# A transformer layer on one core: x times eleven weight blocks as seven products of quarters, interleaved with query/key tiles

## The chip, the cores and the metric

The kernel runs on one core of a Trainium2 chip. The metric is device time in microseconds of one execution. The engines are TensorE (PE, matmuls into PSUM), VectorE (DVE), ScalarE (ACT), GpSimd (POOL) and SyncE (SP, which here only issues transfers). Everything in and out is float32.

## The reference

One layer for 256 tokens of width 2048. `x @ w_in` gives queries, keys and values of three dilated attention groups of eight heads, the queries, keys (1024 columns each), values and output gate (2048 each) of a gated linear attention (GLA), a small decay input, and two gates m_a and m_b of 2048. Both attentions are projected, gated and summed, then follow an output product, a layer norm, a convolutional feed-forward network (FFN) of 5632, and a second layer norm:

```
parts = split(x @ w_in)
o_g, lse_g = dilated attention of group g, 8 heads            # g = 0, 1, 2
ya = (softmax over g of lse_g weighs o_g) @ w_proj_a
o  = GLA(q, k, v, decay), normalised per head
yb = (o * silu(gr)) @ w_proj_b
x1 = layernorm(ALPHA * x + (sigmoid(m_a) * ya + sigmoid(m_b) * yb) @ w_out)
h  = silu(conv3(x1 @ w_gate) + b) * (x1 @ w_up)
out = layernorm(ALPHA * x1 + h @ w_down)
```

## The kernel before

A float32 value is split into two float32r parts, `hi` (ACT copies the value into the narrower type) and `lo` (DVE subtracts `hi` from it), and a product is made of three matmuls: hi by hi, hi by lo, lo by hi. `x` lies split in on-chip memory for the whole first half. Weights come from `wp`, an array of pieces of 128 x 2048 float32 (1 MB) in the order of use. `piece()` (L135) takes the next one: SP loads it into `raw` (three buffers), and `split` (L114) makes `whi` on ACT and `wlo` on DVE (two buffers each).

Two kinds of product use the pieces. In `b16` and `b_tile` (L181 to L193) the weight piece is the stationary operand, for 128 output columns: 16 matmuls of 512 columns (`x` hi and lo side by side, L185) and 16 of 256 columns (L187); `b_sum` (L228) adds the two halves, ACT copying one and DVE adding. In `a_chunk` (L242) x is stationary and the weight moves, 512 output columns for two halves of the tokens: four pieces, 96 matmuls of 512 columns (`a_part`, L238 to L240).

The order is: values `v` of four heads for three groups by `a_chunk`, then 24 query/key tiles `qk` by `b16`, and the same again for the other four heads; 16 tiles `gqk`; `gv` and `gr` (4 chunks each) by `a_chunk`; then for each of four column blocks two `m` chunks (the gates), `yp` (projection a, 8 rows of 128) and `pb` (projection b); `wo`; the first norm; the FFN, in parts FSPLIT = (20, 20, 4) of its 44 blocks, each part's gate and up tiles followed by its share of the down product `wd`; the second norm. Values, queries, keys and results stay on chip.

Smaller work is a list of closures, `side`; `pump()` (L153) takes the next one, after each tile or piece, so that its matmuls fall between the large ones. `attend` (L317) gives a head's bias fetch, scores, softmax, transposes (`turn`) and weighted sums (`mix`), with queries, keys, values and probabilities in split form; `gla` (L473) gives `gate`, `decay`, `keys`, `att` and `outs` of a GLA head, whose last matmuls (`patt`, `pgo`) take plain float32 operands.

The framework sets each engine's order at build time from the order in which instructions are written (an earlier one has priority where both could go) and from when buffers come free, and it writes the waits. Each engine then works through its own list in that order. A tile's buffer, of a tag with a fixed count, is taken again when all that use the older tile are done. PSUM has four banks for large products (`psm`) and four for the rest (`psx`).

## Time and profile before

| | |
|---|---|
| median of 3 runs | 1894.65 us (1894.32 to 1896.28) |
| profiled execution | 1894.34 us; span of its instructions 1892.5 us |
| granted TensorE clock, mean | 0.997 |
| transfers | 359 MB, mean 190 GB/s |

In the rows of the profile, "x" gives a count of instructions and "mean ns" the time of one. Matmuls overlap one another, so that the sum of their durations is more than the time that they take together; the spacing of their starts is read from the chain or the timeline. `<-` names what ended an engine's idle time.

| stage (main product) | from, us | to, us |
|---|---|---|
| v, query/key and gqk tiles, attention | 8.8 | 533.7 |
| gv, with GLA | 533.7 | 650 |
| gr | 650 | 738.8 |
| m, yp, pb | 738.8 | 1047 |
| wo, first norm | 1047 | 1143.2 |
| FFN, last norm | 1143.2 | 1892.5 |

### The profile page before, as it was taken

What the parts mean: (1) busy time and instruction counts of PE and PEld (TensorE: products, weight loads), DVE (VectorE), ACT (ScalarE), POOL (GpSimd) and SP (SyncE); (2) the same over time, 40 slices, a digit from 0 to 9 for tenths busy, and PEclk for the clock granted to TensorE, in tenths of its full rate; (3) what the DMA queues carried; (4) which work ended last, traced back from release to release, by engine and by line L of the source; (5) the groups of instructions that cost most, each with busy time, mean ns of one, the idle gap of its engine ahead of it and who ended that gap; (6) DMA issues with size and microseconds to landing.
All of it is one profiled execution on the core that took longest, in us unless ns stands there. A gap on an engine that the chain in (4) does not pass through costs nothing.

```text
span 1892.5 us, 22845 instructions
## 1 busy us (share of the span) xinstructions
PE 1868.8 (99%) x9510; PEld 1585.6 (84%) x9510; DVE 1098.2 (58%) x1135; ACT 864.2 (46%) x936; POOL 81.0 (4%) x115
## 2 busy tenths in 40 slices
PE   8999999999999999999999999999999999999996
PEld 6888888888877788888888887888888888888885
DVE  5566475665655455445454557766644566664567
ACT  5445445454446544343434435555533455553342
POOL 0000000001000000000000003400000000000001
PEclk9999999999999999999999999999999999999998
DMA  8655545455534455555556654855555655555551
GB/s 283 237 178 180 193 167 193 172 189 181 182 137 155 150 184 181 197 193 187 198 182 219 236 195 145 242 203 190 191 180 198 245 185 194 184 194 185 215 200 67
DMA packets 57618, 359.04 MB, mean 190 GB/s; under 512 B 7089, under 2 KB 8012, under 8 KB 16940
## 3 DMA queue, kind: packets, MB, share of 16 engines
q1 hardware_dynamic: 52908, 345.10, 51.4%
q0 software_dynamic: 4464, 12.24, 2.5%
q8 instruction: 74, 1.21, 0.3%
q10 hardware_dynamic: 144, 0.26, 0.0%
q14 instruction: 28, 0.23, 0.0%
HBM read 355.41 MB, written 3.31 MB: 190 GB/s over the span
## 4 chain that ended last, share of the span: by engine, by line
PE 97%; DVE 2%; ACT 0%; issue 0%; DMA 0%; SPq 0%; ACTq 0%; DVEq 0%
PE qk L185 9%; PE fu L185 8%; PE fg L185 8%; PE qk L187 5%; PE fu L187 4%; PE fg L187 4%; PE wd_t L239 4%; PE wd_t L238 4%; PE wd_t L240 4%; PE gqk L185 3%; PE m_t L239 3%; PE m_t L240 3%; PE m_t L238 3%; PE v_t L238 2%; PE v_t L239 2%; PE v_t L240 2%
## 5 line engine op out<-in xcount | busy, mean ns | idle before, releaser
L116 DVE TENSOR_TENSOR wlo<-raw,whi 128x2048 fp32r<-128x2048 f32 (+1 forms) x336 | 738.8, 2201 | 662.3 <-ACT whi L115 645.7
L115 ACT ACTIVATE whi<-raw 128x2048 fp32r<-128x2048 f32 (+1 forms) x336 | 616.7, 1837 | 560.8 <-PE wd_t L240 107.9
L185 PE MATMUL qk<-x,whi 128*128 128x512 f32 x768 | 184.2, 392 | 0.0
L185 PEld LDWEIGHTS qk<-x,whi 128*128 128x128 f32 x768 | 140.9, 188 | 28.0
L185 PE MATMUL fu<-x,whi 128*128 128x512 f32 x688 | 164.3, 391 | 0.0
L185 PE MATMUL fg<-x,whi 128*128 128x512 f32 x672 | 160.2, 391 | 0.0
L185 PEld LDWEIGHTS fu<-x,whi 128*128 128x128 f32 x688 | 126.4, 188 | 24.5
L185 PEld LDWEIGHTS fg<-x,whi 128*128 128x128 f32 x672 | 123.6, 188 | 24.0
L238 PE MATMUL wd_t<-whi,h 128*128 128x512 f32 x344 | 133.9, 389 | 0.0
L239 PE MATMUL wd_t<-wlo,h 128*128 128x512 f32 x344 | 133.9, 389 | 0.0
L240 PE MATMUL wd_t<-whi,h 128*128 128x512 f32 x344 | 133.8, 389 | 0.0
L187 PEld LDWEIGHTS qk<-x,wlo 128*128 128x128 f32 x768 | 98.5, 191 | 3.8
L238 PE MATMUL m_t<-whi,x 128*128 128x512 f32 x256 | 99.9, 390 | 0.0
L187 PE MATMUL qk<-x,wlo 128*128 128x256 f32 x768 | 99.7, 283 | 0.0
L240 PE MATMUL m_t<-whi,x 128*128 128x512 f32 x256 | 99.6, 389 | 0.0
L239 PE MATMUL m_t<-wlo,x 128*128 128x512 f32 x256 | 99.6, 389 | 0.0
L187 PEld LDWEIGHTS fu<-x,wlo 128*128 128x128 f32 x688 | 88.2, 191 | 3.4
L187 PE MATMUL fu<-x,wlo 128*128 128x256 f32 x688 | 89.2, 283 | 0.0
L187 PEld LDWEIGHTS fg<-x,wlo 128*128 128x128 f32 x672 | 86.2, 191 | 3.3
L187 PE MATMUL fg<-x,wlo 128*128 128x256 f32 x672 | 87.2, 283 | 0.0
L238 PE MATMUL v_t<-whi,x 128*128 128x512 f32 x192 | 75.6, 396 | 1.7 <-ACT whi L115 1.7
L238 PEld LDWEIGHTS wd_t<-whi,h 128*128 128x128 f32 x344 | 64.6, 188 | 13.4
(229 smaller groups left out, 2717.7 us busy)
## 6 DMA issues: line engine op xcount, KB each, us to landing
raw<-in_wp SPq DMA_DIRECT2D x317, 1024.0 KB, 4.8
row<-in_rows POOLq DMA_DIRECT2D x24, 256.0 KB, 5.3
raw<-in_wp SPq DMA_DIRECT2D x20, 256.0 KB, 5.7
bias<-bvd POOLq DMA_DIRECT2D x32, 96.0 KB, 2.8
xraw<-in_xt SPq DMA_DIRECT2D x8, 256.0 KB, 5.7
r<-in_xk POOLq DMA_DIRECT2D x8, 256.0 KB, 5.3
braw<-in_wp SPq DMA_DIRECT2D x8, 256.0 KB, 6.0
out<-r SPq DMA_DIRECT2D x7, 256.0 KB, 2.5
```

The lines of the kernel that those rows point to most:

```text
L115: nc.scalar.activation(hi, src, AF.Copy)
L116: engine.tensor_tensor(lo, src, hi.bitcast(F32), op=ALU.subtract)
L185: nc.tensor.matmul(ps, parts(kc)[0], opnd(kc), start=(kc == 0), stop=False)
L187: nc.tensor.matmul(ps[:, S:], parts(kc)[1], opnd(kc)[:, :S], start=False, stop=(kc == nk - 1))
L238: nc.tensor.matmul(ps, xh, hi, start=first, stop=False)
L239: nc.tensor.matmul(ps, xh, lo, start=False, stop=False)
L240: nc.tensor.matmul(ps, xl, hi, start=False, stop=last)
```

## The change

1. The products of x with the value, gate, `gv` and `gr` columns, eleven blocks of 2048 x 1024 (3, 4, 2 and 2), are made by `seven`: x, tokens by rows of the weight, is cut into quarters A11, A12, A21, A22 and the block into B11, B12, B21, B22 (1024 x 512, two pieces each), and four quarters of the result come from seven products (Winograd's form) instead of eight. Four combinations of x's quarters are made once, by `combine`, on DVE, and split. Those of the weight are made in place on DVE, piece by piece, before the split. Results are combined from PSUM on DVE.
2. These steps (`p1`, `p5`, `p67` twice, `p3`, `p4`, `p2`) alternate with the 64 tiles of queries and keys, one step and one tile, with a `pump` after each, for nine blocks. The two `gr` blocks come last, without tiles; the GLA work is pumped between their steps, two closures for each. What is left of it is issued after them (`drain`).
3. Results no longer stay on chip. `spill` writes them to the chip's DRAM and `fetch` reads them back at the place of use, both through POOL's queue; 256 KB each for most. `m` and `gr` are applied after all products of x are done.
4. Query, key, value and probability are used as float32 in the attention, without a split: one matmul where there were two, and no split of `pT`, `qk` and `v`.
5. Memory: pool `early` is closed after the products of x and `late` opened in its place; x, the combinations, later operands and `h` share eight buffers `res`; `raw` has two buffers, the seven products' pieces have six of their own (`quarter`), `whi` three, `wlo` two; PSUM has two banks for tiles (`psm`), four for `a_chunk` and `seven` (`psc`), two for the rest. POOL's descriptor memory is cut to 4096 bytes a partition.
6. The FFN is cut (16, 16, 8, 4). Its three first pieces, and the last ones of the down product, are no longer prepared ahead in separate blocks.

```diff
-FSPLIT = (20, 20, 4)
+FSPLIT = (16, 16, 8, 4)
...
+    early = ExitStack()
+    now = [early.enter_context(tc.tile_pool(name="early", bufs=1)), (15, 6, 4)]
...
+    def spill(name, src):
+        n_blk[0] += 1
+        d = dpool.tile(list(src.shape), F32, name=f"{name}_{n_blk[0]}")
+        nc.gpsimd.dma_start(d, src)
+        return d
+    def fetch(name, d, make=None):
+        b = (make or blk)(name)
+        nc.gpsimd.dma_start(b, d)
+        return b
...
+    def combine(xs, raw):
+
+        out = [res(f"comb{i}") for i in range(4)]
+        for j in range(4):
+            n_blk[0] += 1
+            f = [tmp("comb").rearrange("p (k t) -> p k t", k=2) for _ in range(4)]
+            (a11, a21), (a12, a22) = ([raw[h][:, :, t * P : (t + 1) * P] for t in range(2)] for h in (j, j + 4))
+            tt = nc.vector.tensor_tensor
+            tt(f[0], a21, a22, op=ALU.subtract)
+            tt(f[1], f[0], a11, op=ALU.subtract)
+            tt(f[2], a11, a21, op=ALU.subtract)
+            tt(f[3], a12, f[1], op=ALU.add)
+            for o, x in zip(out, f):
+                v = o.rearrange("p a (b c) -> p (a b) c", c=S)[:, 2 * j : 2 * j + 2]
+                split(v[:, :, :P], v[:, :, P:], x)
+        return out
+
...
+    def seven(name, xs, comb, i, store):
+
+        st = {}
+        a11 = lambda kc: quarter(xs, kc, 0)
+        a12 = lambda kc: quarter(xs, kc + 8, 0)
+        a22 = lambda kc: quarter(xs, kc + 8, 1)
+        z, s2, s3, s4 = ((lambda kc, c=c: comb_quarter(comb[c], kc)) for c in range(4))
+
+        def part(ps, a, raw, p, first):
+
+            hi, lo = two_parts(raw)
+            for w, which in ((hi, 0), (hi, 1), (lo, 0)):
+                for k in range(4):
+                    kc = 4 * p + k
+                    nc.tensor.matmul(
+                        ps, a(kc)[which], w[:, k * 512 : (k + 1) * 512],
+                        start=(first and w is hi and which == 0 and kc == 0),
+                        stop=(w is lo and kc == 7), skip_group_check=not first,
+                    )
+
+        def product(ps, a, raws, first=True):
+            for p, raw in enumerate(raws):
+                part(ps, a, raw, p, first)
+
+        tt = nc.vector.tensor_tensor
+
+        def add(a, b):
+            tt(a, a, b, op=ALU.add)
+
+        def get(k):
+            return load(i + k, "quarter", 6)
+
+        def p1():
+            st["T"] = [get(0), get(1)]
+            st["A"] = cbank(name + "A")
+            product(st["A"], a11, st["T"])
+            st["s"] = blk("s")
+            nc.scalar.activation(st["s"], st["A"], AF.Copy)
+
+        def p5():
+            st["B12"] = [get(2), get(3)]
+            for a, b in zip(st["T"], st["B12"]):
+                add(a, b)
+            st["D"] = cbank(name + "D")
+            product(st["D"], z, st["T"])
+
+        def p67(p):
+            def f():
+                if not p:
+                    st["B22"] = []
+                    st["B"], st["E"] = cbank(name + "B"), cbank(name + "E")
+                b = get(4 + p)
+                st["B22"].append(b)
+                add(st["T"][p], b)
+                part(st["B"], s2, st["T"][p], p, True)
+                add(st["B12"][p], b)
+                part(st["E"], s3, st["B12"][p], p, True)
+                if p:
+                    add(st["s"], st["B"])
+                    st["u"], c22 = blk("u"), blk("c22")
+                    tt(st["u"], st["s"], st["E"], op=ALU.add)
+                    tt(c22, st["D"], st["u"], op=ALU.subtract)
+                    store(1, 1, c22)
+            return f
+
+        def p3():
+            product(st["D"], s4, st["B22"], first=False)
+            tt(st["s"], st["D"], st["s"], op=ALU.subtract)
+            store(0, 1, st["s"])
+
+        def p4():
+            st["B21"] = [get(6), get(7)]
+            for a, b in zip(st["T"], st["B21"]):
+                add(a, b)
+            product(st["E"], a22, st["T"])
+            add(st["u"], st["E"])
+            store(1, 0, st["u"])
+
+        def p2():
+            product(st["A"], a12, st["B21"], first=False)
+            c = blk("c11")
+            nc.scalar.activation(c, st["A"], AF.Copy)
+            store(0, 0, c)
+
+        return [p1, p5, p67(0), p67(1), p3, p4, p2]
+
...
     def scores(g):
-                q, k = (x[hp] for x in qk[g])
+                q, k = qk[g][:, :S], qk[g][:, S:]
+                ps = bank("ps")
                 for t in range(2):
                     n = (t + 1) * P
-                    ps = bank("ps")
-                    nc.tensor.matmul(ps[:, : 2 * n], q[:, t * P : (t + 1) * P], halves(k)[:, :, :n], start=True, stop=False)
-                    nc.tensor.matmul(ps[:, n : 2 * n], q[:, S + t * P : S + (t + 1) * P], k[:, :n], start=False, stop=True)
+                    pt = ps[:, t * P : t * P + n]
+                    nc.tensor.matmul(pt, q[:, t * P : (t + 1) * P], k[:, :n], start=True, stop=True)
                     s = st["s"][t][:, g * n : (g + 1) * n]
-                    for part, rest in ((ps[:, n : 2 * n], st["T"][:, g, S - n :]), (ps[:, :n], s)):
-                        nc.vector.scalar_tensor_tensor(s, part, scale, rest, op0=ALU.mult, op1=ALU.add)
+                    nc.vector.scalar_tensor_tensor(s, pt, scale, st["T"][:, g, S - n :], op0=ALU.mult, op1=ALU.add)
...
+                nc.tensor.matmul(po, v0, p[:, :S], start=(g == 0), stop=False)
+                nc.tensor.matmul(po[:, P:], v1, p[:, S:], start=False, stop=(g == 2))
...
+    def head(h):
+        qk = [None] * 3
+        bias, scores, rest = attend(h, qk)
+
+        def f(g, which):
+            def t():
+                ps = b16("qk", xop, AT["qk", h] + 2 * g + which)
+                if not which:
+                    qk[g] = blk("qk")
+                b_sum(ps, qk[g][:, which * S : (which + 1) * S])
+                if which:
+                    if not g:
+                        side.append(bias)
+                    side.append(scores[g])
+                    if g == 2:
+                        side.extend(rest)
+            return t
+        return [f(g, which) for g in range(3) for which in range(2)]
+
+    for h in range(NH):
+        tiles.extend(head(h))
+
...
+    with tc.issue_after(loaded.ins):
+        tiles.pop(0)()
+    comb = []
+    tiles.pop(0)()
+    comb.extend(combine(X, XR))
+    steps = []
+    for g in range(3):
+        steps.extend(seven("v", X, comb, AT["v", g], to_v(g)))
+    for u in range(4):
+        steps.extend(seven("m", X, comb, AT["m", u], to(M[u // 2], u % 2)))
+    for u in range(2):
+        steps.extend(seven("gv", X, comb, AT["gv", u], to(GV, u)))
+    late = []
+    for u in range(2):
+        late.extend(seven("gr", X, comb, AT["gr", u], to(GR, u)))
+    ratio = len(tiles) / len(steps)
+    done = 0
+    for n, step in enumerate(steps):
+        step()
+        pump()
+        while done < (n + 1) * ratio and tiles:
+            tiles.pop(0)()
+            done += 1
+            pump()
+
...
     for h in range(GH):
         stages, o = gla(h)
-        side.extend(stages)
-        GV.append(evacuate("gv", a_chunk("gv", xop, 16, n_pump=2)))
-        side.append(o)
+        side.extend([*stages, o])
+    for step in late:
+        step()
+        pump(2)
     drain()
+    early.close()
+    now[:] = ctx.enter_context(tc.tile_pool(name="late", bufs=1)), (17, 10, 1)
...
+    YA2 = [res("ya") for _ in range(2)]
+    for h in range(NH):
+        y = YA2[h // 4][:, h % 4]
+        split(y[:, :S], y[:, S:], fetch("yaf", YA[h], tmp))
...
+        ws = [by_cols(piece(i)) for i in idx]
...
-    nc = bacc.Bacc("TRN2", target_bir_lowering=False, num_devices=1)
+    nc = bacc.Bacc("TRN2", target_bir_lowering=False, num_devices=1, dynamic_dma_scratch_size=4096)
```

More of the change, by code (lines that the diff above doesn't have):

```diff
@@ L378, in f @@
-                nc.tensor.matmul(po[:, S + P :], v1[1], p[:, 0, S:], start=False, stop=(g == 2))
-                if g == 2:
-                    f32 = tmp("yaf")
-                    b_sum(po, f32)
-                    y = blk("ya", F32R)
-                    split(y[:, :S], y[:, S:], f32)
-                    YA[h] = y
-            return f
-        return bias, [scores(g) for g in range(3)], [soft(0), soft(1), turn(0), turn(1), mix(0), turn(2), mix(1), mix(2)]
-    def both(a, b):
-        for x, y in zip(a, b):
-            side.extend([x, y])
@@ L645, in hybrid_layer @@
     R = [[], []]
-    stats = [tpool.tile([P, 4, 6], F32, tag=f"st{t}", name=f"st{t}", bufs=1) for t in range(2)]
+    stats = [now[0].tile([P, 4, 6], F32, tag=f"st{t}", name=f"st{t}", bufs=1) for t in range(2)]
     def mean_and_scale(t):
```

444 lines of the change are left out of this document (223 added, 221 removed).

## The prediction

> **What bounds the kernel now.** I read the page's busy times first, then what TensorE (PE) waited for, then busy time by stage.
>
> ```profile
> span 1892.5 us, 22845 instructions
> PE 1868.8 (99%) x9510; PEld 1585.6 (84%) x9510; DVE 1098.2 (58%) x1135; ACT 864.2 (46%) x936; POOL 81.0 (4%) x115
> ...
> PE pbias L301 <- DMA oh<-in_onehot: 3.1, 1, 3.1
> PE v_t L238 <- ACT whi L115: 1.7, 1, 1.7
> ...
> core 0: us, PE busy (x) PEld busy (x) DVE busy (x) ACT busy (x) POOL busy (x), PEclk, DMA share, GB/s
> 8.80:533.70 524.90, 524.89 (x2888) 457.62 (x2889) 320.98 (x418) 253.88 (x303) 22.24 (x42) 1.00 0.56 196
> 533.70:650.00 116.30, 115.97 (x535) 89.68 (x534) 63.47 (x73) 66.94 (x107) 1.63 (x4) 1.00 0.41 145
> 738.80:1047.00 308.20, 308.20 (x1377) 255.56 (x1376) 149.31 (x89) 121.81 (x83) 2.19 (x4) 1.00 0.55 195
> 1876.40:1892.50 16.10, 0.03 (x1) 0.00 (x0) 10.56 (x14) 1.31 (x3) 4.20 (x3) 0.59 0.36 130
> ```
>
> From 8.8 to 1876 us PE never stops; its longest waits are 3.1 and 1.7 us, both at the start. The other engines are hidden beneath it, so time comes off only by taking PE work away, and the change can lose time only by making PE wait. VectorE (DVE), at 58%, is next in line.
>
> **What the change takes from PE.** Busy time is no price here, because matmuls overlap. The spacing is:
>
> ```profile
> 26.15:47.90 21.75, 21.75 (x97) 18.02 (x96) 1.38 (x2) 1.18 (x2) 1.00 0.72 254
> ...
> 195.02 1.92 PE qk L187 x16
> 196.94 0.11 PE ppt L360
> 197.05 0.22 PE ppt L363 x2
> 197.27 3.65 PE qk L185 x16
> ...
> L238 PE MATMUL m_t<-whi,x 128*128 128x512 f32 x256 | 99.9, 390 | 0.0
> L238 PE MATMUL v_t<-whi,x 128*128 128x512 f32 x192 | 75.6, 396 | 1.7 <-ACT whi L115 1.7
> L238 PE MATMUL gv_t<-whi,x 128*128 128x512 f32 x128 | 50.6, 395 | 0.0
> L238 PE MATMUL gr_t<-whi,x 128*128 128x512 f32 x128 | 50.1, 391 | 0.0
> ```
>
> One 512-column matmul every 21.75/96 = 0.2267 us (the first row is the v_t tile alone); one query/key tile is 3.65 + 1.92 = 5.57 us. The eleven blocks are these four tiles: (256+192+128+128) x 3 lines = 2112 matmuls, 192 a block. Seven products of quarters are 7 x 8 x 3 = 168 a block, 1848 in all. The 264 saved are 59.9 us.
>
> Float32 attention changes PE little. The float32 product that exists already is `pgo`, at two records a matmul:
>
> ```profile
> 570.33 1.72 PE pgo L558 x4
> 572.05 0.86 PE pgo L560 x2
> ...
> 114.89 0.12 PE ps L337
> 115.02 0.06 PE ps L338
> 115.08 0.29 PE ps L337
> 115.37 0.12 PE ps L338
> ```
>
> 512 columns cost 0.86 us, so 256 + 128 columns cost 0.645 us, against 0.59 in the last four rows. `mix` has the same column counts as those rows, 0.53 at the spacings above (0.2267 + 0.12 + 0.12 + 0.06). So +0.05 and +0.12, 24 times: +4 us. The profiled execution is 1894.34 us (span plus 1.8; the median of the runs shown is 1894.65), so with PE as full as now: 1894.34 - 59.9 + 4 = 1838.5 us. The rest of the sum is PE waiting.
>
> **What it puts on DVE.**
>
> ```profile
> L116 DVE TENSOR_TENSOR wlo<-raw,whi 128x2048 fp32r<-128x2048 f32 x316 | 725.6, 2296 | 656.8 <-ACT whi L115 640.3 <-ACT pa L230 9.5 <-PE ps L337 4.1
> L115 ACT ACTIVATE whi<-raw 128x2048 fp32r<-128x2048 f32 x316 | 604.6, 1913 | 553.2 <-PE wd_t L240 107.9 <-PE m_t L240 85.3 <-PE gqk L185 46.0
> L608 DVE TENSOR_TENSOR sg<-sg,gr_t 128x512 f32<-128x512 f32 x8 | 5.5, 688 | 4.7 <-ACT sg L607 4.6
> ...
> 197.05 2.29 DVE L116 TENSOR_TENSOR wlo<-raw,whi 128x2048 fp32r<-128x2048 f32 x1 [2.36 <-ACT whi L115]
> 199.26 0.42 DVE L231 TENSOR_TENSOR qkf<-qk,pa 128x256 f32<-128x256 f32 x1
> 199.60 0.55 DVE L116 TENSOR_TENSOR pT<-ppt,pT 128x384 fp32r<-128x384 f32 x1
> ...
> 75.80:533.70 457.90, 10.62 (x72) 8.43 (x72) 46.53 (x128) 13.12 (x32) 1.00 0.52 183
> 533.70:650.00 116.30, 38.02 (x18) 0.00 (x0) 1.00 0.41 145
> ...
> 639.23 0.63 PE patt L541 x4
> 648.59 0.86 PE pgo L560 x2
> ```
>
> Start to start, a 128x2048 operation is 2.21 us and a 128x256 one 0.34; a 128x512 one I take at 0.61 (0.69 less the same 0.08). The seven products turn the 8 splits of a block into 14 and add 8 sums of weight quarters of the same shape (twice two in `p67`, two each in `p5` and `p4`; in place, taken at the split's price), and 5 sums of 128x512 results: 22 x 2.21 + 5 x 0.61 = 51.7 us a block, where PE needs 38.1.
>
> Main loop (nine blocks' 63 steps in turn with the 64 tiles). DVE: 9 x 51.7 = 465; tiles 64 x 2.55 = 163; attention 29 (the tile `s` row, 46.5 us, without its 48 of 96 score additions, for seven heads); `combine` and x, 32 operations of 0.34 and 8 of 0.61, 16. That is 673 us. PE: 64 x 5.57 + 63 x 5.44 + 7 heads x 5 (0.645 x 6 + 0.33 x 3) = 734 us. DVE stands at 92%. ACT has 1.91 a split, so about 60%. Within a block DVE needs, with its tile, 7.5 us in `p1`, 12 in `p5` and in the first `p67`, 14 in the second, 8 in `p3`, 12.5 in `p4`, 7.5 in `p2`, against 11.7 on PE each time. It falls behind by about 3 us and gets it back. Two `wlo` buffers let it be one piece ahead, and a piece's low part is needed only after its high-part matmuls (1.8 us for a quarter, 3.65 for a tile), so the 3 us are covered. I put 8 us (1%) on waits that line up badly; ends 0 and 60.
>
> Late stage (the two `gr` blocks, with `gla` between the steps and no tiles). DVE: 2 x 51.7 + 25.4 for `gla` (63.47 less the splits' 38.02 in the window 533.7 to 650) + 4 for the last head = 133 us. PE: 76 for 28 quarters, 29 for `gla` and `pgl` (116.3 less 384 x 0.2267), 5 for the last head = 110. Here DVE is the bound: +23 us. The side list adds more: it gives 13 steps for each head's 12 chances, so some 16 are left for this stage; with 20 of `gla` against 28 chances, 8 remain when the last product is issued, and the last heads' chain (`keys`, `att`, `outs`) runs after it with little beside it. The last two rows show that chain for the last head now: from its first `patt` to its last `pgo` 10.2 us; with about half of a head's 6.4 us of DVE ahead of it, and the second head partly behind the first, some 16 us, of which a part fills gaps: +12 (ends 5 and 25).
>
> Then `early` closes, and all that `late` holds lies where it lay. If its first buffer waits for the last of `early`, the last `spill` must land, and `yaf` be fetched and split, before `yp` can start:
>
> ```profile
> r<-in_xk POOLq DMA_DIRECT2D x8, 256.0 KB, 5.3
> out<-r SPq DMA_DIRECT2D x7, 256.0 KB, 2.5
> raw<-in_wp SPq DMA_DIRECT2D x317, 1024.0 KB, 4.8
> POOL r L702 <- DMA row<-in_rows: 29.4, 8, 4.4
> ...
> 0.00:20.00 20.00, 15.19 (x48) 9.80 (x49) 10.18 (x17) 11.55 (x18) 2.80 (x15) 1.00 0.86 280
> ```
>
> 2.5 + 5.3 + issue and split about 2: +10 us (ends 0, if buffers are reused one by one, and 13). POOL has some 150 such transfers where it had 74, each of them ahead of its need by a step (11 us) in the main loop, and the PE steps behind it wait only if that lead is gone: I take 0, end 30. The fourth row shows such a wait, 4.4 us at the longest.
>
> Start. At 280 GB/s the first tile needs all of x and one piece, 3 MB in 11 us, then 1 MB for 5.6 us of PE, then 2 MB for p1; before, 1.5 MB fed each 5.4 us. PE has done some 5.6 us where it had done 9 by 18 us, waits 3 for the second piece, and `combine` (11 us of small operations ahead of p1's low parts) takes 1 or 2 more: +8 (ends 4 and 14). FFN's three first pieces are split after the norm, 5.7 us of ACT, where one of them was ready before it: +2 (ends 0 and 5). FSPLIT with one part more leaves the matmul count, and adds 8 accumulations of 0.69 on an idle DVE: 0. SP's weight loads keep their bytes: blocks load 8 MB as before.
>
> **Sum:** 1838.5 + 8 + 8 + (23 + 12 + 10) + 2 = 1901.5, so 1902 us, 0.4% above now. The saving on PE is real and is paid back, mostly in the two last blocks.
>
> **A rule that speaks against it.** The clock row: over the idle end (1876.4 to 1892.5) PE was granted 0.59, and 1.00 in every busy stage shown. The Trainium skill, "TensorE: Matmul & The Clock Gate", Part 1, says that the clock falls to half after an idle window of about 3.4 us and takes as long of work to come back. The trace agrees with the first half; no row shows a short stall. By that rule only the wait at the change of pools is long enough, an estimate of 2 us more, 1904.
>
> **Rivals.**
> 1. *The waits are filled: faster.* The order is set ahead of time, and an operation emitted later may fill a gap. If `late` reuses buffers one by one, `yp` (42 us of PE) covers the chain of `gla` and its spill; then the late stage costs 23 + 5, the start 4, the main loop 3, FFN 0: 1838.5 + 35 = 1874, up to 1890 with half of the rest. For it: DVE has 61 us of slack in the main loop, and before it never held PE. It decides when the losses stay under 52 us in all. 0.36.
> 2. *DVE bounds the main loop too: much slower.* It has 262 large operations in 734 us and 61 us of slack, 0.23 us each. Before, each split waited 640/316 = 2 us for its high part; that cost nothing with 42% idle. If 0.45 us of it stays for each, PE loses 262 x 0.45 - 61 = 57 us more: 1959. Against it: sums and the tile's split can be put between. 0.14.
> 3. *Spills and fetches hold PE through POOL's queue,* which is in order: 30 us more, 1932. 0.07.
> 4. *The clock goes to half in the late stage,* where PE stops often though briefly: its 110 us become 220, 87 over DVE's 133: 1989. The page's rule would need longer gaps than 1 to 2 us. 0.03.
>
> **How the numbers follow.** My own case, 1892 to 1918, has 0.40; it is the likeliest. 0.2% (3.8 us) is about what a measurement of this kernel can tell from no change, so its lowest part, 1892 to 1898.4, is "same": 0.13. Faster 0.36 is rival 1; slower the remaining 0.51. The range 1866 to 1945 leaves out the bottom of rival 1, the upper part of 2, and 4: under 0.2. The likeliest case's own range is 1892 to 1918.
>
> **What would show it.** PE's matmul count in the eleven blocks 264 lower at 0.227 us; DVE near 1430 us busy. The main loop at 92% DVE with PE full would hold the fourth term; idle PE there behind `wlo` is rival 2. In the two `gr` blocks PE waits for `wlo` with DVE full. A PE gap of over 8 us ahead of `yp`, behind `ya`'s split and a fetch, is the pool term; no gap is rival 1. I am wrong if the late stage takes under 120 us or the main loop over 780.

## The result, and the profile after

The changed kernel takes 1960.9 us (median; 1959.6 to 1962.5) where the kernel before takes 1895.1 (1894.3 to 1896.3): 1.0347 times as long, 95% interval 1.0329 to 1.0365. The forecast was 1902 with a range of 1866 to 1945. The profiled execution took 1961.5 us. Its page, with the rows that answer to those of before:

```profile
span 1959.8 us, 22945 instructions
...
PE 1859.2 (95%) x9246; PEld 1558.6 (80%) x9246; DVE 1428.3 (73%) x1225; ACT 973.5 (50%) x951; POOL 161.9 (8%) x261
...
PE   7999999999999999885799998899999999999997
...
DVE  7898988989898898994555556666545666446557
...
PEclk9999999999999999887799999899999999999998
...
L137 DVE TENSOR_TENSOR wlo<-raw,whi 128x2048 fp32r<-128x2048 f32 (+1 forms) x239 | 545.0, 2281 | 216.8 <-PE wd_t L245 53.3 <-issue 36.0 <-PE fg L214 35.4
...
L137 DVE TENSOR_TENSOR wlo<-quarter,whi 128x2048 fp32r<-128x2048 f32 x154 | 351.6, 2285 | 58.9 <-ACT whi L136 43.0 <-issue 4.2 <-PE qk L214 3.8
...
L321 DVE TENSOR_TENSOR quarter<-quarter,quarter 128x2048 f32<-128x2048 f32 x88 | 200.0, 2284 | 0.5
```

PE has exactly the 264 matmuls less that were counted (9510 to 9246), and DVE is at 1428 us, as forecast. But PE's busy time fell by 9.6 us only, where the matmuls and the attention together should have taken off 56, and its idle time grew from 24 to 101 us. Lost time thus shows in two places: as idle, and as busy time in which the same work takes longer, in part at a lower clock. The slices say where: the first, and then four from about 780 to 980 us, where PE drops to 5 and the clock to 7, and less of it at the norm and the start of the FFN (8 from 1176 to 1274 us).

The waits of PE, longest sums first (in total, times, longest), and the busy time by stage:

```profile
PE patt L689 <- DVE xk L665: 19.3, 3, 10.6
PE yp_t L244 <- ACT ya L136: 8.8, 1, 8.8
PE gqk L212 <- ACT whi L136: 5.7, 3, 3.1
PE pgo L707 <- POOL att L697: 5.7, 3, 3.5
PE vD L308 <- ACT whi L136: 4.7, 1, 4.7
PE fu L212 <- DVE yb L237: 4.6, 1, 4.6
```

```profile
core 0: us, PE busy (x) PEld busy (x) DVE busy (x) ACT busy (x) POOL busy (x), PEclk, DMA share, GB/s
0.00:100.00 100.00, 82.42 (x365) 63.81 (x366) 81.94 (x84) 52.33 (x56) 6.53 (x18) 0.95 0.66 244
100.00:765.70 665.70, 665.70 (x3425) 568.28 (x3424) 602.07 (x422) 374.99 (x302) 55.99 (x96) 1.00 0.62 223
765.70:892.00 126.30, 109.96 (x462) 83.82 (x460) 119.52 (x94) 73.31 (x78) 18.26 (x34) 0.91 0.36 129
892.00:954.50 62.50, 25.98 (x63) 14.77 (x63) 17.67 (x31) 21.45 (x52) 15.96 (x28) 0.61 0.30 108
954.50:1006.20 51.70, 50.64 (x225) 41.12 (x226) 38.36 (x47) 35.43 (x48) 18.80 (x36) 0.95 0.89 316
...
1184.30:1196.50 12.20, 7.62 (x24) 3.28 (x22) 8.02 (x16) 9.58 (x15) 0.00 (x0) 0.82 0.32 119
1196.50:1945.40 748.90, 739.20 (x3891) 636.29 (x3890) 453.54 (x455) 339.35 (x360) 37.88 (x41) 0.99 0.53 188
```

The stages are: start; main loop; the two `gr` blocks; from the last product of `gr` to the first of `yp` (I call it the gap); `yp`; the first norm; the FFN. The main loop keeps PE full with DVE at 90% (602.07 of 665.70). The gap has 62.5 us with 26 of PE, 18 of DVE and 21 of ACT: here nobody is busy. The norm took 8.3 us before and 12.2 now, the FFN 733.2 and 748.9.

What the gap waits for stands in its timeline (start, duration, engine, operation; in brackets the idle time before it and what ended it):

```profile
890.55 4.49 DVE L137 TENSOR_TENSOR wlo<-raw,whi 128x2048 fp32r<-128x2048 f32 x2
...
891.21 4.08 POOL L697 TENSOR_SCALAR_AFFINE_SELECT att<-att 128x256 f32<-128x256 f32 x1 [3.09 <-ACT att L695]
...
909.19 0.54 POOL L109 DMA_DIRECT2D sp<-c  x1 [4.33 <-ACT c L375]
910.24 1.07 POOL L114 DMA_DIRECT2D gq<-gkqs  x2 [0.51 <-issue]
...
913.31 0.69 DVE L659 SCALAR_TENSOR_TENSOR gq<-gq,ge 128x512 f32<-128x512 f32 x1 [2.14 <-DMA gq<-gkqs]
...
914.72 1.97 PE L689 MATMUL patt<-gq,xk 128*128 128x64 f32 x8 [10.55 <-DVE xk L665]
919.85 0.40 POOL L697 TENSOR_SCALAR_AFFINE_SELECT att<-att 128x256 f32<-128x256 f32 x1 [8.01 <-ACT att L695]
...
924.81 1.18 PE L630 MATMUL pz<-glp,gwp 80*128 80x256 f32 x1
...
928.16 0.55 POOL L109 DMA_DIRECT2D os<-o  x1 [2.86 <-DVE o L716]
928.70 1.07 POOL L114 DMA_DIRECT2D gq<-gkqs  x2
...
933.15 0.69 DVE L659 SCALAR_TENSOR_TENSOR gq<-gq,ge 128x512 f32<-128x512 f32 x1
...
934.55 1.97 PE L689 MATMUL patt<-gq,xk 128*128 128x64 f32 x8 [6.67 <-DVE xk L665]
...
948.06 0.55 POOL L109 DMA_DIRECT2D os<-o  x1 [2.86 <-DVE o L716]
950.92 0.17 POOL L733 MEMSET gbuf<- 128x2 f32 x3 [2.32 <-DMA os<-o]
951.43 4.25 POOL L114 DMA_DIRECT2D yaf<-yas  x8 [0.34 <-issue]
...
954.50 0.79 PE L244 MATMUL yp_t<-whi,ya 128*128 128x512 f32 x1 [8.81 <-ACT ya L136]
```

Two whole GLA heads are left after the last product, and they run one after the other, 20 us apart (`patt` at 914.7 and 934.6). A head's `gq` is issued on POOL's queue behind the writes ahead of it (`sp` in the first case, the last `os` of the head before in the second). The rows show what that costs here: DVE's operation on `gq` waits 2.14 us for the fetch in the first of the two heads, and in the second it does not wait for it, as it starts where ACT's `ge` has just ended. The rest of the 20 us is the head's own series of small operations. It begins with `pz` (924.8 in the second head, right behind the last `pgo` of the head before), takes 9.7 us to `patt`, and 11.1 more to the end of its last `pgo` at 945.7. Then comes the change of pools as the prediction had it: last write, memset at the place it frees, fetch, split, `yp`.

### The profile page after: what moved, and what is told of

Same layout as the page of the kernel before. It is cut to its first block, busy times and chain, and to the rows that moved or that the text cites. A ratio compares the mean times of both kernels' runs of the same rounds, so it can differ in the third digit from the quotient of the medians.

```text
span 1959.8 us, 22945 instructions
## 1 busy us (share of the span) xinstructions
PE 1859.2 (95%) x9246; PEld 1558.6 (80%) x9246; DVE 1428.3 (73%) x1225; ACT 973.5 (50%) x951; POOL 161.9 (8%) x261
## 4 chain that ended last, share of the span: by engine, by line
PE 47%; DVE 3%; issue 3%; DMA 2%; ACT 1%; POOL 1%; POOLq 0%; DVEq 0%; ACTq 0%; SPq 0%
PE fu L212 8%; PE fg L212 8%; PE fu L214 4%; PE fg L214 4%; PE wd_t L244 4%; PE wd_t L246 4%; PE wd_t L245 4%; DMA raw<-in_wp 2%; PE wo_t L246 1%; PE wo_t L244 1%; PE wo_t L245 1%; DVE wlo L137 1%; PE pb_t L245 1%; PE pb_t L244 1%; PE pb_t L246 1%
## 5 line engine op out<-in xcount | busy, mean ns | idle before, releaser
L137 DVE TENSOR_TENSOR wlo<-raw,whi 128x2048 fp32r<-128x2048 f32 (+1 forms) x239 | 545.0, 2281 | 216.8 <-PE wd_t L245 53.3
L136 ACT ACTIVATE whi<-raw 128x2048 fp32r<-128x2048 f32 (+1 forms) x239 | 452.7, 1894 | 485.7 <-DMA raw<-in_wp 374.8
L136 ACT ACTIVATE whi<-quarter 128x2048 fp32r<-128x2048 f32 x154 | 293.3, 1916 | 218.4 <-DVE quarter L321 120.0
L137 DVE TENSOR_TENSOR wlo<-quarter,whi 128x2048 fp32r<-128x2048 f32 x154 | 351.6, 2285 | 58.9 <-ACT whi L136 43.0
L321 DVE TENSOR_TENSOR quarter<-quarter,quarter 128x2048 f32<-128x2048 f32 x88 | 200.0, 2284 | 0.5
L212 PE MATMUL qk<-x,whi 128*128 128x512 f32 x768 | 189.1, 396 | 0.0
L244 PE MATMUL wd_t<-whi,h 128*128 128x512 f32 x352 | 137.1, 390 | 0.0
L246 PE MATMUL wd_t<-whi,h 128*128 128x512 f32 x352 | 137.0, 389 | 0.0
L244 PEld LDWEIGHTS wd_t<-whi,h 128*128 128x128 f32 x352 | 66.1, 188 | 13.9 <-ACT h L136 0.4
L246 PEld LDWEIGHTS wd_t<-whi,h 128*128 128x128 f32 x352 | 66.1, 188 | 13.8 <-DVE h L137 0.2
```

The lines of the kernel that those rows point to most:

```text
L136: nc.scalar.activation(hi, src, AF.Copy)
L137: nc.vector.tensor_tensor(lo, src, hi.bitcast(F32), op=ALU.subtract)
L212: nc.tensor.matmul(ps, parts(kc)[0], opnd(kc), start=(kc == 0), stop=False)
L244: nc.tensor.matmul(ps, xh, hi, start=first, stop=False)
L246: nc.tensor.matmul(ps, xl, hi, start=False, stop=last)
L321: tt(a, a, b, op=ALU.add)
```

## The experiments

The theory after this reading: the loss is a chain, not an engine, two GLA heads in series and then the change of pools; and smaller waits at the start, the norm and the FFN. The rival: DVE, which the sums and second splits fill, is the cause of most of it. (The letters in the quoted expectations are each run's own.)

Stage lengths, in us, from start to start of the matmuls named (gap: from the last product of `gr` to the first of `yp`; norm: last `wo` to first `fg`; FFN: first `fg` to last `wd`). Each is from one profiled execution. In the nine runs from gr_plain to start4, none of which changes the FFN's own work, the FFN lies between 743.5 and 748.9, so a few us in that column are not clear of the spread:

| kernel | median | gr | gap | norm | FFN |
|---|---|---|---|---|---|
| changed | 1960.9 | 125.8 | 63.0 | 12.4 | 748.5 |
| gr_plain | 1944.9 | 120.4 | 50.6 | 12.4 | 747.0 |
| no_sums | 1929.0 | 111.1 | 63.5 | 12.7 | 743.5 |
| ya_ahead | 1945.0 | 126.8 | covered | 12.4 | 747.4 |
| spread | 1937.4 | mixed | 18.0 | 12.3 | 746.5 |
| gp_banks | 1943.7 | 117.9 | 51.5 | 12.4 | 746.8 |
| gp_pump3 | 1925.8 | 119.7 | 34.3 | 12.4 | 748.6 |
| gp_ahead | 1924.0 | 121.0 | 34.0 | 12.4 | 745.9 |
| gp_all | 1913.2 | 125.4 | 17.2 | 12.4 | 746.2 |
| start4 | 1955.1 | 134.1 | 46.8 | 12.4 | 748.9 |
| gains_late | 1961.5 | 125.0 | 64.3 | 12.3 | 747.5 |
| best1 | 1898.2 | 129.9 | 0.2 | 12.0 | 747.4 |
| ffn_banks | 1952.9 | 125.2 | 64.4 | 12.4 | 740.2 |
| gains_dve | 1957.8 | 125.8 | 63.5 | 12.3 | 745.4 |
| norm_first | 1957.7 | 125.6 | 62.9 | 9.4 | 749.9 |
| ffn_raw | 1960.3 | 131.2 | 58.9 | 12.0 | 744.6 |
| best2 | 1889.8 | 128.3 | 0.3 | 9.4 | 741.8 |
| best3 | 1890.7 | 133.0 | 0.2 | 9.4 | 733.9 |

### Is it DVE?

**gr_plain**: the two `gr` blocks by four plain chunks, as before, with two closures to a piece.

```diff
-        late.extend(seven("gr", X, comb, AT["gr", u], to(GR, u)))
...
+    for h in range(GH):
+        pss = a_chunk("gr", xop, 16, AT["gr", h], 2)
```

> The two gr blocks by plain a_chunk (64 matmuls more per the two blocks... 48 in all, +10.9 us of PE; 16 splits in place of 28 splits, 16 sums and 10 result sums: DVE -68 us), everything else as in the change. Theory A (DVE is full in the last two blocks, so the queued GLA work comes late and is left for the end): the stretch from the first gr matmul to the first yp matmul falls from 189 us to about 135 to 145 (PE 121, a short remainder, the pool change 9), total about 1910 to 1918. Theory B (the end is made by the GLA chain and POOL's queue whatever DVE does): the 54 us after the last gr matmul stay, the total is 1950 to 1965.

1944.9 us, between the two theories. DVE's work in the stage was halved, from 119.5 to 57.7 us busy:

```profile
767.40:888.20 120.80, 114.79 (x518) 89.77 (x516) 57.73 (x61) 58.52 (x82) 20.57 (x39) 0.97 0.57 201
888.20:938.40 50.20, 19.67 (x54) 12.68 (x54) 13.47 (x27) 16.73 (x40) 10.04 (x22) 0.59 0.29 98
```

The stage shortened by 5 us (PE has 48 matmuls more to do in it, 11 us), the gap by 12, and 50 us of it stay with no engine full. DVE is part of the loss, not most of it.

**no_sums**: the 88 sums of weight quarters (L321) are left out, so that the products are of other operands; all else runs as in the changed kernel.

```diff
-            for a, b in zip(st["T"], st["B12"]):
-                add(a, b)
```

> The 88 in-place sums of weight quarters are left out of all eleven blocks (so the seven products are of other operands than they should be); DVE loses 194 us, the matmuls stay. Theory A (DVE decides in the gr blocks only): the main loop stays near 757 us from 8.9 to its end (at most 10 us less), the gr blocks fall from 126 to about 95 to 100 us, the GLA remainder shrinks by 10 to 20: total 1905 to 1925. Rival C (DVE holds PE in the main loop as well, through waits that are spread thin): the main loop falls by 20 us or more, total under 1900. Theory B: total about 1935, from the gr blocks alone.

1929.0, 32 us less, between the times that theories A and B gave. The places of 29 of them are clear: the main loop ends 14.5 us earlier, all of it won in the first 100 us, where PE is busy 91.6 us instead of 82.4 with 73 matmuls more (438 for 365), and the `gr` stage is 14.7 shorter. The main loop behind 100 us has the same pace with the sums (665.70 us for 3425 matmuls) and without (651.20 for 3352), and the gap does not move. The FFN, which has no such sums, is 5 us shorter in this run; nothing shows why.

```profile
0.00:100.00 100.00, 91.63 (x438) 73.93 (x439) 76.90 (x84) 62.77 (x63) 7.67 (x20) 1.00 0.78 291
100.00:751.20 651.20, 651.20 (x3352) 555.26 (x3351) 454.17 (x349) 368.31 (x295) 54.84 (x94) 1.00 0.62 221
```

DVE thus costs about 15 us at the start and 15 in the `gr` blocks, and nothing in the 666 us between, although it is 90% busy there.

**spread**: the 64 tiles go on through the `gr` steps instead of ending before them.

```diff
-    ratio = len(tiles) / len(steps)
+    ratio = len(tiles) / (len(steps) + len(late))
```

> The 64 tiles are spread over all 77 steps, the gr blocks included, and two closures are pumped after each step and each tile there. Theory A: DVE has 97% of PE's time in the first nine blocks (673 less 31 us against 734 less 68) and 90% in the last two; the stretch up to yp falls from 954 to about 900 to 915, total 1907 to 1921. Rival C (DVE at 97% already stalls PE): no gain in the last stage that the first nine blocks do not lose, total over 1945.

1937.4. The gap falls to 18 us, but PE now waits in the stage itself (`grD` for DVE's `c` 6.0, `ppt` for `s` 7.1), since the closures of the attention come late. The time lies between the two theories. That the order of the closures binds here is argued from these waits; gp_pump3 tests it in a simpler kernel.

### Is it the chain of GLA?

The four runs here start from gr_plain (the diff has one place of each edit). **gp_pump3** is gr_plain with three closures to a piece instead of two; **gp_ahead** is gr_plain with q, k and v of all four heads fetched at the start of the stage into the free `quarter` buffers; **gp_banks** gives `pz` and `patt` PSUM banks of `psm` instead of `psx`; **gp_all** has all three.

```diff
-        pss = a_chunk("gr", xop, 16, AT["gr", h], 2)
+        pss = a_chunk("gr", xop, 16, AT["gr", h], 3)
...
-            q, k = (fetch("gq", GKQ[i][h]) for i in (1, 0))
+            q, k = HQ[h][:2]
...
-            pz = bank("pz")
+            pz = mbank("pz")
```

> The gr blocks by plain chunks (1944.9 us, where 50 us lie between the last gr matmul and the first yp matmul), with three closures pumped after each piece in place of two. Theory D1 (GLA is left over because some 16 attention closures stand before it in the list): GLA starts about 15 us sooner and all its closures are issued four pieces (21 us of PE) before the end; the 50 us fall to about 25 to 30, total 1920 to 1925. Theory D2 (the heads go one after another because buffers or POOL's queue hold the next one): they come sooner in the list but not on the engines, total above 1938.

> As gr_plain, with the four heads' q, k and v of GLA fetched ahead of the GLA closures into the free quarter buffers: four of the 15 blk buffers a head are no longer taken, and no fetch of GLA stands behind a spill in POOL's queue. Theory D2 (buffers and the queue): the waits of patt for xk (20.6 us) fall below 8, the 50 us to about 30, total 1922 to 1930. Theory D1 (list order alone): less than 6 us.

> As gr_plain, with the banks of pz and patt taken from the two of the tiles, which are idle there, so that pgo has the two of psx alone. If the two banks hold the next head's gate back: 8 to 15 us lower, 1930 to 1937. If buffers or the list do it: within 4 us of 1945.

> All three together. If the end is made by these three alone, only the change of pools (9 us) and the last head's spill remain after the last gr matmul: 15 us where there were 50, total 1908 to 1912. If the remainder is the DVE and ACT chain of the heads itself: above 1925.

gp_pump3 gives 1925.8 (1920 to 1925 if the list was it), gp_ahead 1924.0 (1922 to 1930 if buffers and queue were): each takes some 16 us off the gap, by another road (fewer closures left, or shorter ones). gp_banks gives 1943.7, and its two times (1941.0 and 1946.3) lie around gr_plain's: no gain from the banks can be seen. With them the last head's `pz` starts at 892.2 instead of 902.9, but its `patt` at 916.9 instead of 919.7. Together 1913.2, just over the 1908 to 1912 expected, and the gap is 17.2 us, of which 11.5 are the change of pools:

```profile
PE yp_t L244 <- ACT ya L136: 11.5, 1, 11.5
...
893.50:910.30 16.80, 2.85 (x7) 1.07 (x7) 3.63 (x4) 6.71 (x15) 8.72 (x16) 0.73 0.51 181
```

With the fetches ahead, 17 of gr_plain's 51 us went: `patt` of the last two heads is 17.8 us apart (883.0 and 900.8) where it was 27.3 (892.4 and 919.7). In gr_plain the fetch of the last head stands in POOL's queue behind a write (`sp`) that waits for ACT, and DVE then waits for the fetch:

```profile
912.46 0.54 POOL L109 DMA_DIRECT2D sp<-c  x1 [5.71 <-ACT c L726]
...
916.74 0.69 DVE L657 SCALAR_TENSOR_TENSOR gq<-gq,ge 128x512 f32<-128x512 f32 x1 [5.52 <-DMA gq<-gkqs]
```

So in gr_plain the fetches are a large part of a head's time. (gp_ahead also takes four of the fifteen `blk` buffers that a head uses off it, and no run separates these buffers from the queue.) But gp_pump3, which leaves the fetches as they were, has 17.7 us between the last two heads (881.6 and 899.3): that is the price of a head that does not wait for its `gq`. In the changed kernel, at 19.8, the fetches are therefore some 2 us of a head, and the rest is the head itself. The change of pools shows as one wait of 9 to 12 us in each of these runs.

**ya_ahead**: on the changed kernel, `yp`'s operand is fetched ahead into a `quarter` buffer, and two chunks of `yp` are issued before the rest of GLA.

```diff
+    yps = [a_chunk("yp", yop, 8, AT["pa"] + 2 * n, 2) for n in range(2)]
     drain()
     early.close()
```

> The operand of projection a is fetched into a weight buffer and split before the pools change, and two of the four yp chunks (21.8 us of PE) are issued ahead of the rest of GLA. If PE idles at the end because nothing else may be issued (pool change and GLA chain), these 21.8 us go into the gaps and the 8.8 us wait ahead of yp goes for two chunks: total 22 to 30 us lower, 1931 to 1939. If the chain of GLA is itself lengthened by the yp work between (in-order engines), less than 15 us.

1945.0, 16 us less, between the two expectations. PE works in the gap, and the 8.8 us wait is gone, but a wait of 11.3 for the gate `m`, which `late` must still fetch after the change of pools, takes its place ahead of the third chunk.

### The start, the attention, and POOL in the FFN

**start4**: four tiles ahead of the first step instead of two.

```diff
-    tiles.pop(0)()
+    for _ in range(3):
+        tiles.pop(0)()
```

> The change, with four tiles instead of two ahead of the first step. If the 18 us that PE loses in the first 100 us come from the first seven products needing 2 MB a step and DVE's 11 us of combine before their low parts, then two tiles more (11 us of PE for 2 MB) cover part of it: the 4.7 us wait of vD goes, 5 to 9 us lower, 1952 to 1956. If they come from loading x and the first pieces alone (3 MB ahead of the first tile), nothing changes: within 2 us of 1961.

1955.1, in the range expected and for another reason: PE is busy 82.9 of the first 100 us (82.4 in the changed kernel), the main loop ends at 767.8 (765.7), `gr` takes 8 us more and the gap 16 less, as the third head starts 9.6 us ahead of the last product's end (`pz` at 892.7, the end at 902.3) where it started 9.4 behind it. The start was not helped; what its loss hangs on, no_sums showed.

**f32_only**: the kernel before, with the float32 attention alone.

```diff
-        nc.tensor.matmul(ps[:, : 2 * n], q[:, t * P : (t + 1) * P], halves(k)[:, :, :n], start=True, stop=False)
...
+        nc.tensor.matmul(pt, q[:, t * P : (t + 1) * P], k[:, :n], start=True, stop=True)
```

> The kernel before, with float32 attention alone (query, key, value and probability without a split). PE as worked out: +4 us; DVE loses about 50 us, which PE does not wait for. Total 1896 to 1901. If DVE's or ACT's relief mattered anywhere: below 1894.

1899.7, 1.0026 times the kernel before (1.0017 to 1.0035), so +4.9 us, where +4 was forecast. DVE is freed of 55 us in the first stage (266.38 busy where it was 320.98), and nobody waits less for it:

```profile
8.80:533.70 524.90, 524.74 (x2856) 454.36 (x2856) 266.38 (x274) 231.40 (x245) 22.14 (x42) 1.00 0.55 194
```

**gains_late**: seven empty closures ahead of the FFN's gains, so that POOL would do them later.

```diff
+    side.extend([lambda: None] * 7)
     side.extend(gain(n, t) for n in range(4) for t in range(2))
```

> The change, with the eight gain closures (POOL multiplies and adds on the residual) seven tiles later in the first FFN part. If POOL's reads slow DVE's two-input operations where FFN starts (a 256-column operation of 0.42 to 0.51 us is 1.5 us there) and PE waits for them, the stretch from the first fg matmul to 1260 us shrinks by 5 to 9 us: 1952 to 1956. If FFN's start waits for its pieces to be split after the norm: within 2 us of 1961.

1961.5, no change, and no test either: the gains ran at the same time as before, as the first gain starts at 1202.9 where it had started at 1201.9. The question was taken up again by gains_dve.

**best1** puts gp_all, ya_ahead, start4 and gains_late together, with `yp`'s operand fetched ahead of the last `gr` chunks.

> gp_all (1913.2) with the operand of projection a fetched ahead and two yp chunks under the rest of GLA (the 11.5 us wait ahead of yp), with the gains later (5 to 9 us) and four tiles first (5 to 9 us). If these add up: 1884 to 1895, no slower than the kernel before. If the waits only move on to the next thing, as the 11.3 us for the gate did in ya_ahead: 1900 to 1908.

1898.2, 1.0016 times the kernel before (1.0006 to 1.0025): the gap is closed (0.2 us) and 63 us have come back, at a time between the two expectations, but norm and FFN still take 12.0 and 747.4.

### Norm and FFN

The instructions there are nearly the same in both kernels (one part more, and pieces that are no longer prepared ahead); banks, buffers and order differ. In the changed kernel's first FFN blocks, DVE's and POOL's rows:

```profile
1215.79 3.41 DVE L137 TENSOR_TENSOR wlo<-raw,whi 128x2048 fp32r<-128x2048 f32 x1 [4.42 <-PE fg L231]
...
1217.55 2.81 POOL L874 TENSOR_TENSOR r<-r,row 128x512 f32<-128x512 f32 x1
...
1222.42 1.50 DVE L900 SCALAR_TENSOR_TENSOR gr<-gbuf,prm,gr 128x256 f32<-128x256 f32 x1
...
1224.16 1.30 POOL L874 TENSOR_TENSOR r<-r,row 128x512 f32<-128x512 f32 x1
...
1232.94 4.53 DVE L137 TENSOR_TENSOR wlo<-raw,whi 128x2048 fp32r<-128x2048 f32 x1
```

A split takes 3.4 to 4.5 us instead of 2.3 beside POOL's gains, and a gain 2.8 instead of 1.3.

**ffn_banks**: the first twelve `fg` and `fu` blocks take their accumulators from `psc`'s four banks (the first three did so already).

```diff
-            ps = ... b16("fg", x1op, at)
+            ps = ... b16("fg", x1op, at, get=cbank if f < 6 else None)
```

> The changed kernel with the accumulators of the FFN's first six columns (fg and fu) taken from the four banks of psc, instead of the two of psm. Theory B (banks: the FFN's first blocks wait 4.6 us for a bank that VectorE has not read out, since psm has two banks where it had four): that wait goes and first fg to last wd shrinks from 749 to 739-744 us, so 1951-1956. Theory C (the banks only show that VectorE is late; its two-input operations are slow there, 3.4 to 4.5 us for 2048 columns, beside GpSimd's gains): the wait turns up at a later split, 1959-1962.

**gains_dve**: the gains on DVE.

```diff
-            nc.gpsimd.tensor_tensor(a, a, row(2, n), op=ALU.mult)
+            nc.vector.tensor_tensor(a, a, row(2, n), op=ALU.mult)
```

> The changed kernel with the sixteen gain multiplications and additions ahead of the FFN's output on VectorE instead of GpSimd. Theory C (GpSimd's two-input operations hold VectorE's up between 1196 and 1240): the 2048-column splits there take 2.3 us again, the fu wait of 4.6 us goes, VectorE has some 16 x 0.65 = 10 us of work more that lies beside the products, and the kernel takes 1951-1956. Theory B (banks alone): the added work makes VectorE later still, 1961-1970.

**norm_first**: DVE's splits of the first three FFN pieces are issued behind the norm's last operation on DVE.

```diff
-        ws = [by_cols(piece(i)) for i in idx]
+        with tc.issue_after(made[1].ins):
+            ws = [by_cols(piece(i)) for i in idx]
```

> The changed kernel with VectorE's part of the splits of the FFN's first three blocks held behind the last operation of the normalisation's scale. Theory N (the 2.28 us split that ran between the last chunk's residual and its statistics is in the chain of the norm): from the last product of wo to the first of fg takes 9.5-10.5 us instead of 12.2, and 1958.5-1960 in all. Rival: the split that is put off is the one that the first fg products' second half or the third block then waits for, and the time is given back at 1200-1210: 1960-1962.

**ffn_raw**: the FFN's pieces are loaded into the six `quarter` buffers instead of the two `raw`.

```diff
-            return two_parts(load(i))
+            return two_parts(load(i, *ring))
```

> The changed kernel with the FFN's weight blocks loaded into the six buffers that the quarters had used, instead of the two of raw (before, there were three). Theory R (with two buffers a load starts only when VectorE has read the block before the last, so a late VectorE makes the load, ScalarE's split and the product late in turn): the waits of fu and fg behind yb and whi, 7 us in sum, go or halve, and first fg to last wd takes 738-744 us where it took 748.5; 1950-1956. Rival (the loads are early enough, and only banks and GpSimd matter): 1959-1962.

ffn_banks takes 1952.9 us: the FFN is 8.3 us shorter, and the wait of `fu` for `yb` is gone, as theory B of that run had it. gains_dve takes 1957.8: every split is 2.28 us again (the row at the same place below), the FFN is 3.1 shorter, less than expected, as `fg` now waits 6.2 us for ACT's `whi`. norm_first takes 1957.7: the norm is 3.0 shorter, and the FFN gives 1.4 back. Of the medians, ffn_banks alone is clear of the changed kernel's (1.0290 to 1.0320 times the kernel before, against 1.0329 to 1.0365); the intervals of gains_dve and norm_first overlap it. What shows these two are the lengths of the splits and of the norm, which is 12.0 to 12.7 us in every other version of the changed kernel without that edit.

```profile
1213.36 2.28 DVE L137 TENSOR_TENSOR wlo<-raw,whi 128x2048 fp32r<-128x2048 f32 x1
```

ffn_raw takes 1960.3, no gain, though the FFN is 3.9 shorter and its `fg` no longer waits for `whi` (`fu` now waits 6.1 us for `yb`, where it waited 4.6): `gr` is 5.4 longer, as in best3.

**best2** is best1 without the empty closures and with ffn_banks, gains_dve and norm_first; **best3** is best2 with ffn_raw.

> The version with all measures so far (gr by plain chunks, three closures to a piece, GLA's operands and projection a's operand fetched ahead, separate banks in GLA, two chunks of projection a ahead of the drain, four tiles ahead of the first step), which took 1898, with the three edits of this call: banks, gains on VectorE, the norm's chain first. If both B and C hold: 1884-1890, under the kernel before (1895). If one of them is idle: 1889-1894. If neither does anything: 1896-1900.

> The last version (1890, with banks, gains on VectorE and the norm's chain first) with the FFN's loads in six buffers as well. It still showed a wait of 6.1 us of fg for ScalarE's whi, which itself waited 6.6 us for a load. Theory R: that wait goes, 1882-1887. Rival: it is passed on to VectorE's part of the split, 1888-1892.

best2 takes 1889.8 us, 0.9975 times the kernel before (0.9966 to 0.9984). It is a quarter of a per cent faster than the kernel before, and 3.6% faster than the changed one. best3 takes 1890.7, 0.9974 (0.9962 to 0.9985). Its FFN is down to 733.9, 1.1 over the kernel before (732.8 from start to start): banks, POOL's gains and the two `raw` buffers together are nearly the whole loss there. How it divides among them is known only roughly, as each length is from one execution. Neither expectation had the rest: in the window of the `gr` stage, best2 first and best3 second, 30 GB/s more flow, and that stage and `yp` give back what the FFN won (+4.7 and +2.2 us).

```profile
766.00:896.00 130.00, 124.05 (x570) 95.45 (x569) 73.39 (x94) 75.95 (x126) 21.55 (x42) 0.99 0.53 183
```

```profile
766.00:896.00 130.00, 122.03 (x550) 94.01 (x549) 72.18 (x93) 74.22 (x125) 20.50 (x40) 0.96 0.61 213
```

SP's queue of best3 says what flows: the first and the last of the FFN's six loads into `quarter`, 377 and 248 us before the first `fg` at 1140.3. That these loads slow the stage is argued: it is some 5 us longer in both pairs (ffn_raw and best3), PE's waits in it grew by 2.8 us (for `wlo` 3.3 to 4.8, for `xk` 1.3 to 2.6), and no run holds the loads back.

```profile
762.83 0.33 SPq L144 DMA_DIRECT2D quarter<-in_wp  x1
...
892.47 0.33 SPq L144 DMA_DIRECT2D quarter<-in_wp  x1
```

## Why the prediction was wrong

The sign and the bound were right, and the time was 59 us over. Step by step:

- *The saving on PE, 59.9 us.* Right in the count, 264 matmuls; no run takes it alone, but best2, with 48 of them put back, still ends below the kernel before.
- *Float32 attention, +4.* Right: +4.9 alone.
- *DVE's total, near 1430.* Right: 1428.
- *Main loop, +8.* Nothing was lost there behind 100 us. The reasoning (DVE at 92%, small leads covered by two `wlo` buffers) held; rival 2 is false.
- *Start, +8.* Missized. With 0 to 765.7 where the sum would end near 759 (8.8 + 734 + 16), the two terms together are short by about 7. In the first 100 us PE is idle 17.6, where it was 4.8 before; DVE is the reason (no_sums gives 14.5 back), not the loads that the prediction counted first.
- *Late stage, 23 + 12 + 10.* This step failed. By the prediction's own sum the stage from the last tile to the first `yp` takes 110 + 45 = 155 us; it took 188.8. The part for DVE was of the right size: 23 forecast, and about 16 came back without the seven products (gr_plain's stage, 5 us shorter with 11 of PE's work more). The pool term was right: 8.8 us of wait for 10. What was missized is the 12 for the rest of GLA. The prediction priced a head by the 10.2 us from `patt` to the last `pgo`, added about 3 for DVE's work ahead of them, and let the second head run partly behind the first. The 10.2 was right (11.1 in the gap). But ahead of `patt` a head has the series of `gate`, `decay` and `keys`, 13.4 and 9.7 us from `pz` to `patt` in the gap, and the heads did not overlap at all: two of them, with the end of a third, filled 53.8 us from the last product to the last `pgo`. The kernel before showed both, had the head been read from `pz` on:

```profile
626.77 0.68 PE L483 MATMUL pz<-glp,gwp 80*128 80x256 f32 x1
```

From here to the last `pgo` (649.4) are 22.6 us, and the head before had its own last `pgo` until 627.3. Other products hid this there. Why the heads do not overlap stays open: gp_banks let `pz` start earlier, and `patt` hardly followed. POOL's queue, which the prediction named only as a rival for the main loop, is a small part: waits of 2.1 us for `gq` and 1.9 for `gv` in the gap.
- *The clock.* The granted clock fell to 0.61 in the gap, and to 0.91 in the `gr` blocks (rows above). The Trainium skill, "TensorE: Matmul & The Clock Gate", Part 1, has the clock fall to half after an idle window of about 3.4 us; the gap agrees, with 0.50 granted over the wait of 10.6 us and still 0.50 behind it (914.7 to 921.0). The prediction allowed 2 us for it by that rule, for the one wait that it foresaw. PE was busy 26 us in the gap with 63 matmul records, so the lower clock is a part of it that the prediction had no place for; no run takes it by itself.
- *`yp`, 0.* By my estimate it needed about 47 us (192 matmuls at 0.2267 are 43.5, and there are transposes beside them), and it took 51.7, at 316 GB/s, beside the fetches of the gates; no run tests what held it.
- *FFN and norm, +2.* This failed too: +4 and +15.7. The prediction looked for changed instructions and found three splits. It did not ask what the fewer banks (`psm` four to two) and `raw` buffers (three to two), listed in the change, do to a stage that is not edited. ffn_banks, gains_dve, norm_first and ffn_raw gave back 8.3, 3.1, 3.0 and 3.9 us in their stages, of which the 3.1 and 3.9 are hardly clear of the spread; with all four, best3 is within 2 us of the kernel before in both stages.
- *Rivals.* Rival 1 (waits filled, 1874 to 1890) is what best2 comes to at 1889.8: the price is not in the algorithm. But it took some ten edits, of which one gives part of the saving back. Rival 3's mechanism, POOL's queue, had a small part at another place, and a larger one in gr_plain; rival 4's clock loss was real at a smaller size.

Added up: 7 at the start, 34 in the late stage, 4 in `yp`, 18 in norm and FFN (4 + 15.7 less the 2 allowed), and 2 less at the end (14.4 us after the last product where it was 16.1): 61, where the miss is 59. The 2 us between them are within the rounding of these estimates.

## What to carry to other kernels

A saving on the engine that bounds is kept only while every stage has other work ready for that engine; count what is left over at the end of an interleaved loop in whole dependent chains, price a chain from its first operation to its last, with its fetches, and look in the trace whether one chain starts before the one ahead of it has ended. A change that shares out memory anew must be costed in all stages that use those buffers and banks, edited or not: here nearly a third of the miss lay in code whose instructions had hardly changed. And more buffers for a later stage start its loads earlier: here an earlier stage became 5 us longer with them.

## What the runs showed of the hardware

- VectorE and GpSimd hold each other up. A mask operation of GpSimd (`AFFINE_SELECT`, 128 x 256) took 4.08 us, until the second of two splits of VectorE had ended (891.2 to 895.3 beside 890.6 to 895.0), and 0.40 otherwise; a split took up to 4.53 us beside GpSimd's gains and 2.28 without them, a 256-column operation 1.50 against 0.48. The Trainium skill, "SBUF — State Buffer", "Who interferes with whom", says that an operation of VectorE with two inputs in SBUF contends with one of GpSimd that reads SBUF, because its second input comes through a read interface that the two share; these rows agree, and gains_dve shows the times of the FFN's splits without it. Why the mask operation did not get in between the two splits no run shows.
- VectorE at 90% busy cost TensorE nothing over 666 us of a regular schedule: 0.194 us a matmul with the sums of weight quarters (665.70 for 3425) and without them, at 70% (651.20 for 3352).
